# A hybrid decoder trunk: seven start offsets, 0 to 96 bytes, for the split weights in SBUF

## The chip, the cores and the metric

The kernel runs on one core of a Trainium2 chip. The metric is the device time of one execution in microseconds (us): a median of 1567.96 over 3 runs, which lie between 1567.52 and 1570.27.

## What is computed

Two layers, each: a half-step SwiGLU FFN, a token-mixing sub-layer (a Mamba-2 SSD branch and a gated DeltaNet branch on the same normalised input), and another half-step FFN. All of it is float32, for 256 tokens of width 1024:

```python
h = h + 0.5 * swiglu(rms_norm(h, ffn1_norm[l]), ffn1_w_in[l], ffn1_w_out[l])
u = rms_norm(h, mix_norm[l])
(z_s, xbc, dt_s, qkv, z_d, b_d, a_d, gate_s, gate_d) = jnp.split(u @ w_in[l], split_points, axis=-1)
y_s = mamba2_branch(z_s, xbc, dt_s, ...)
y_d = deltanet_branch(qkv, z_d, b_d, a_d, ...)
merged = (jax.nn.sigmoid(gate_s) * (y_s @ ssm_w_branch[l])
          + jax.nn.sigmoid(gate_d) * (y_d @ dn_w_branch[l]))
h = h + merged @ w_out[l]
h = h + 0.5 * swiglu(rms_norm(h, ffn2_norm[l]), ffn2_w_in[l], ffn2_w_out[l])
```

What matters here are the products with the weights: `u @ w_in`, the two FFN matrices, and the three output matrices.

## The kernel before, in words

**Split weights.** A float32 product is made from products of type fp32r. Each operand is split into a high part (the value copied into a tile of type fp32r) and a low part (the value minus its high part). A product then takes three matmuls: high by high, high by low, low by high. The weights come from HBM in half units of 128 partitions x 1024 float32 (512 KB). `load` (line 140) issues the DMA of one on the SP queue, into one of 5 `wraw` buffers, or for the first of each group of FFN output blocks into a slot (`wfirst`). `prep` (line 149) then splits a half unit: ScalarE (ACT) copies it to `hi` (line 162), VectorE (DVE) subtracts to get `lo` (line 169). `hi` and `lo` are tiles `whi` and `wlo` with NSPL = 5 buffers each. For the FFN output blocks `prep` also forms differences of half units in place (lines 163 to 171). `take` (line 181) hands out the next pair and keeps 5 pairs split ahead and the loads a few further ahead; the order is that of a plan (lines 99 to 133), and an order written out by hand (`ORDER`, line 44) for the mixer. ACT, DVE and POOL helpers are at lines 65 to 77, so most operations show lines 66 (ACT), 69 and 72 (DVE).

**The users of the split weights** are four kinds of matmul groups:

- `tok_chunk` (line 296, matmuls at lines 287 to 289 through `mm3`): the normalised input uT is stationary, the weights stream as the moving operand, 512 columns. Tiles `t` and `f`.
- `out_chunks` and `block_products` (lines 353 and 391, the same lines 287 to 289): gate products or branch outputs (`gh`/`gl`, `mh`/`ml`, `bh`/`bl`, block sums) are stationary, the weights stream, 512 columns. Tiles `o`, `b` and `p`.
- `chan_chunk` (line 313, lines 292 to 294 through `mm3w`): the weights are stationary (128x128 pieces), uT streams, 256 columns. Tiles `kk`, `qq`, `vv`, `zd`, `bc`, `xs`.
- `chan_pair` (line 332, lines 342 and 346): the FFN's input product. The high weights are stationary for 512 columns (the high and the low part of uT together), the low weights for 256.

Every matmul is preceded by a weight load (LDWEIGHTS, PEld in the profile) of its stationary operand; TensorE issues the load of the next weights while the current matmul streams.

**Placing.** Tiles are allocated pool by pool along the partition: constants, h and uT; then the pool of the weights (`wraw`, `whi`, `wlo`); then the slots (`gh`, `gl`, `mh`, ...); then small temporaries (`bh`, `bl`, ...). Each `whi` and `wlo` buffer has 4096 bytes per partition and starts on a multiple of 128 bytes. uT starts at byte 32928, which is 32 more than a multiple of 64.

Of the kernel before, what the change touches and what calls it, by code (L numbers as in the profile page):

```python
# [8 lines left out]
F32R = mybir.dt.float32r  # L9
I32 = mybir.dt.int32  # L10
AF = mybir.ActivationFunctionType
ALU = mybir.AluOpType
# [4 lines left out]
P = 128  # L17
# [13 lines left out]
NSPL = 5  # L31
# [20 lines left out]
def trunk_kernel(ctx, tc, x, wst, wsm, norms, lpar, rpar, cst, out):  # L52
# [4 lines left out]
    wpool = ctx.enter_context(tc.tile_pool(name="wpool", bufs=1))  # L57
# [7 lines left out]
    def act(o, i, func=AF.Copy, **kw):  # L65
        return A.activation(out=o, in_=i, func=func, **kw)  # L66

    def tt(o, a, b, op):
        return V.tensor_tensor(out=o, in0=a, in1=b, op=op)  # L69
# [9 lines left out]
    def f(ap):  # L79
        return ap.bitcast(F32)  # L80
# [67 lines left out]

    def prep(i):
        kind, js, _ = plan[i]  # L150
        hi = wpool.tile([P, 1024], F32R, tag="whi", name="whi", bufs=NSPL)
        lo = wpool.tile([P, 1024], F32R, tag="wlo", name="wlo", bufs=NSPL)

        def less(o, a, b):
            tt(raws[js[o]][:], raws[js[a]][:], raws[js[b]][:], ALU.subtract)


        r = raws[js[{"q2": 1, "q4": 4, "q5": 3}.get(kind, 0)]]
        with ExitStack() as behind:
            for ins in state["behind"].pop(i, ()):  # L160
                behind.enter_context(tc.issue_after(ins))
            act(hi[:], r[:])
            if kind == "q1":
                less(1, 2, 1)
            elif kind == "q2":
                less(0, 2, 0)
            elif kind == "q4":
                less(0, 3, 0)
            tt(lo[:], r[:], f(hi[:]), ALU.subtract)
            if kind == "q0":  # L170
                less(0, 1, 0)
        for o in {"d": (0,), "q2": (1,), "q3": (2,), "q4": (4,), "q5": (3,), "q6": (0,)}.get(kind, ()):
            raws.pop(js[o])
        halves[i] = (hi, lo)
# [6 lines left out]
    def take():  # L181
        j = state["taken"]
        state["taken"] = j + 1
        ahead("loaded", min(plan[min(j + NSPL, n_forms) - 1][2] + NRAW - 1, n_raw), load)
        ahead("prepped", min(j + 1 if state["hold"] else j + NSPL, n_forms), prep)
        return halves.pop(j)
# [46 lines left out]
    def rstd_of(t):  # L233

        ss = small([P, 2], "ss")
        for n in range(2):
            junk = tmp2("junk")
            state["square"] = act(junk[:], h[:, t, n * 512 : (n + 1) * 512], AF.Square, scale=1.0 / 32.0, accum_out=ss[:, n : n + 1])
        z = small([P, 2], "zz")
        ts(z[:, 0:1], ss[:, 0:1], ss[:, 1:2], ALU.add, EPS, ALU.add)  # L240
        rsqrt(z[:, 1:2], z[:, 0:1], [P, 1])
        return z[:, 1:2]
# [18 lines left out]
    def norm_in(nw, add=None):  # L261

        for t in range(2):
            with tc.high_priority(offset=PRI), ExitStack() as behind:
                if add:
                    add(t)
                    if t == 0:
                        behind.enter_context(tc.issue_after(state["sums"][5].ins))
                ins, done = rms_chain(t, nw)
            if t == 0:  # L270
                state["hold"] = False
                n = state["taken"]
                if not add:
                    ahead("prepped", n + 1, prep)
                    with tc.issue_after(done[0].ins), tc.issue_after(done[1].ins):
                        ahead("prepped", n + START, prep)
                with tc.issue_after(ins.ins):
                    ahead("prepped", n + 2, prep)
                if add:
                    state["behind"][n + 2] = [d.ins for d in done]  # L280
            elif add:

                state["behind"][n + 4] = (state["square"].ins, ins.ins)
                state["input"] = done
# [946 lines left out]
    for t in range(2):  # L1231
# [5 lines left out]
        r = rstd_of(t)  # L1237
# [137 lines left out]
```

## Time and profile before

| what | value |
|---|---|
| median of 3 runs | 1567.96 us |
| span of the profiled execution, from first to last instruction | 1565.8 us |
| PE matmul busy | 1545.0 us |
| PEld (weight loads) busy | 1342.0 us |
| DVE busy | 1302.4 us |
| ACT busy | 999.8 us |
| POOL busy | 53.2 us |
| DMA: bytes, mean rate | 292.99 MB, 187 GB/s |
| mean granted TensorE clock | 0.999 |

The profiled execution has no time of its own beside its span; the runs' median lies 2.2 us above the span. Busy times are sums over instructions. PE's instructions are pipelined, so their busy time overlaps that of the next; the distance from the start of one to the start of the next, the pitch, is what a stream of matmuls costs. A row of the timeline holds the start in us from the span's beginning, the time taken, the engine, line, operation, output and inputs, and the shape.

### The profile page before, as it was taken

The numbers are of one execution on the slowest core, as the hardware profiler recorded it, in microseconds if no ns is written. First come the engines' busy times: TensorE is split into PE (matmuls) and PEld (weight loads), VectorE is DVE, ScalarE is ACT, GpSimd is POOL, SyncE is SP. The second block draws the span as 40 slices with busy tenths as digits, with TensorE's granted clock in tenths as the row PEclk, the third lists the DMA queues.
The fourth block names the chain that finished last, engine by engine and source line by source line (L and its number), as shares of the span: only waits on it lengthen the run. The fifth ranks groups of instructions, "written<-read, shape, count | busy, mean of one in ns | idle before, by whom it ended". The sixth has DMA issues, their size and how long they took to land.

```text
span 1565.8 us, 26672 instructions
## 1 busy us (share of the span) xinstructions
PE 1545.0 (99%) x10152; PEld 1342.0 (86%) x10152; DVE 1302.4 (83%) x2048; ACT 999.8 (64%) x1694; POOL 53.2 (3%) x60
## 2 busy tenths in 40 slices
PE   8999999999999999999999999999999999999998
PEld 6888779999888888888788887899998888888886
DVE  6889969957899766899878998699579996679897
ACT  6666668766675655666566676686656666466664
POOL 0000010000000000000000001010000000000000
PEclk9999999999999999999999999999999999999999
DMA  8565565553455555465765566555336546555553
GB/s 298 197 214 188 195 212 173 178 158 118 174 207 173 177 205 196 159 210 177 262 204 187 168 198 223 189 189 189 116 123 213 177 166 212 201 175 166 198 189 134
DMA packets 94215, 292.99 MB, mean 187 GB/s; under 512 B 22325, under 2 KB 23301, under 8 KB 93062
## 3 DMA queue, kind: packets, MB, share of 16 engines
q1 hardware_dynamic: 94086, 291.29, 55.2%
q8 instruction: 79, 1.29, 0.3%
q14 instruction: 50, 0.41, 0.1%
HBM read 289.33 MB, written 1.92 MB: 186 GB/s over the span
## 4 chain that ended last, share of the span: by engine, by line
PE 76%; DVE 13%; DMA 5%; issue 3%; ACT 2%; POOL 1%; SPq 0%; POOLq 0%; DVEq 0%; ACTq 0%
PE fc L342 15%; PE fc L346 8%; DVE wlo L69 7%; PE t L287 3%; PE t L288 3%; PE t L289 3%; DMA wraw<-in_wst_dram 3%; PE b L289 3%; PE b L288 3%; PE b L287 2%; PE xs L292 2%; PE xs L293 2%; PE xs L294 2%; PE o L288 1%; PE o L289 1%
## 5 line engine op out<-in xcount | busy, mean ns | idle before, releaser
L69 DVE TENSOR_TENSOR wlo<-wraw,whi 128x1024 fp32r<-128x1024 f32 x488 | 591.0, 1221 | 139.8 <-ACT whi L66 136.1
L66 ACT ACTIVATE whi<-wraw 128x1024 fp32r<-128x1024 f32 x488 | 511.6, 1057 | 176.4 <-PE b L289 29.8
L342 PE MATMUL fc<-uT,whi 128*128 128x512 f32 x1280 | 445.5, 391 | 0.0
L346 PE MATMUL fc<-uT,wlo 128*128 128x256 f32 x1280 | 360.9, 282 | 0.0
L342 PEld LDWEIGHTS fc<-uT,whi 128*128 128x128 f32 x1280 | 240.3, 188 | 50.7
L346 PEld LDWEIGHTS fc<-uT,wlo 128*128 128x128 f32 x1280 | 241.8, 189 | 0.8
L287 PE MATMUL t<-whi,uT 128*128 128x512 f32 x256 | 102.9, 403 | 0.0
L288 PE MATMUL t<-wlo,uT 128*128 128x512 f32 x256 | 101.5, 396 | 0.2 <-DVE wlo L69 0.2
L289 PE MATMUL t<-whi,uT 128*128 128x512 f32 x256 | 101.5, 397 | 0.0
L66 ACT ACTIVATE whi<-wfirst 128x1024 fp32r<-128x1024 f32 x64 | 67.8, 1059 | 29.7 <-DVE wfirst L69 20.4
L66 ACT ACTIVATE sg<-fc 128x256 f32<-128x256 f32 x80 | 30.6, 382 | 82.3 <-PE fc L346 82.3
L69 DVE TENSOR_TENSOR wlo<-wfirst,whi 128x1024 fp32r<-128x1024 f32 x64 | 78.1, 1220 | 2.0 <-ACT whi L66 1.9
L287 PE MATMUL b<-whi,bh 128*128 128x512 f32 x192 | 76.1, 398 | 0.0
L288 PE MATMUL b<-wlo,bh 128*128 128x512 f32 x192 | 74.9, 390 | 0.0
L289 PE MATMUL b<-whi,bl 128*128 128x512 f32 x192 | 74.3, 394 | 0.3 <-DVE bl L69 0.3
L292 PE MATMUL xs<-uT,whi 128*128 128x256 f32 x256 | 73.1, 286 | 0.0
L294 PE MATMUL xs<-uT,wlo 128*128 128x256 f32 x256 | 71.6, 280 | 0.0
L293 PE MATMUL xs<-uT,whi 128*128 128x256 f32 x256 | 71.4, 279 | 0.0
L288 PE MATMUL o<-wlo,gh 128*128 128x512 f32 x160 | 64.6, 404 | 2.6 <-DVE wlo L69 2.5
L69 DVE TENSOR_TENSOR wfirst<-wraw,wfirst 128x1024 f32<-128x1024 f32 x48 | 58.6, 1220 | 8.9 <-DMA wraw<-in_wst_dram 8.9
L289 PE MATMUL o<-whi,gl 128*128 128x512 f32 x160 | 62.5, 391 | 0.0
L287 PE MATMUL o<-whi,gh 128*128 128x512 f32 x160 | 62.1, 392 | 0.0
(317 smaller groups left out, 3424.5 us busy)
## 6 DMA issues: line engine op xcount, KB each, us to landing
wraw<-in_wst_dram SPq DMA_DIRECT2D x504, 512.0 KB, 4.5
wfirst<-in_wst_dram SPq DMA_DIRECT2D x16, 512.0 KB, 5.8
dc<-rdram SPq DMA_DIRECT2D x8, 1024.0 KB, 8.4
nw<-in_norms_dram SPq DMA_DIRECT2D x6, 512.0 KB, 6.2
gb<-rdram SPq DMA_DIRECT2D x8, 256.0 KB, 5.3
h<-in_x_dram SPq DMA_DIRECT2D x4, 256.0 KB, 5.7
out_dram<-fo SPq DMA_DIRECT2D x4, 256.0 KB, 2.1
dq<-X SPq DMA_DIRECT2D x2, 256.0 KB, 5.0
```

Source lines behind the costliest of these rows:

```text
L66: return A.activation(out=o, in_=i, func=func, **kw)
L69: return V.tensor_tensor(out=o, in0=a, in1=b, op=op)
L287: PE.matmul(ps, lh, rh, start=start, stop=False)
L288: PE.matmul(ps, lh, rl, start=False, stop=False)
L289: return PE.matmul(ps, ll, rh, start=False, stop=stop)
L292: PE.matmul(ps, wh, mh, start=start, stop=False)
L293: PE.matmul(ps, wh, ml, start=False, stop=False)
L294: PE.matmul(ps, wl, mh, start=False, stop=stop)
L342: PE.matmul(ps[a][:], wh[:, c0 : c0 + P], uT[:, kt].rearrange("p o t -> p (o t)"), start=kt == 0, stop=False,)
L346: PE.matmul(ps[a][:, 0:S], wl[:, c0 : c0 + P], uTh[:, kt, :], start=False, stop=kt == KT - 1)
```

## The change

The `whi` and `wlo` buffers get 24 elements (96 bytes) more per partition, and the 1024 elements in use start at an offset into the buffer: 16 bytes times (i mod 7) for the high part and 16 bytes times ((i div 7) mod 7) for the low part, where i counts the half units split so far. So the high part goes through 0, 16, ..., 96 bytes with each half unit, and the low part changes every seventh. The buffers are 4192 bytes apart instead of 4096, so they no longer all start on a multiple of 128; the slots and temporaries behind them move by 960 bytes. `hi` and `lo` are now views of the tiles, so the later uses lose their `[:]`.

```diff
     def prep(i):
         kind, js, _ = plan[i]
-        hi = wpool.tile([P, 1024], F32R, tag="whi", name="whi", bufs=NSPL)
-        lo = wpool.tile([P, 1024], F32R, tag="wlo", name="wlo", bufs=NSPL)
+        o1, o2 = 4 * (i % 7), 4 * (i // 7 % 7)
+        hi = wpool.tile([P, 1024 + 24], F32R, tag="whi", name="whi", bufs=NSPL)[:, o1 : o1 + 1024]
+        lo = wpool.tile([P, 1024 + 24], F32R, tag="wlo", name="wlo", bufs=NSPL)[:, o2 : o2 + 1024]
...
-            act(hi[:], r[:])
+            act(hi, r[:])
...
-            tt(lo[:], r[:], f(hi[:]), ALU.subtract)
+            tt(lo, r[:], f(hi), ALU.subtract)
```

## The prediction

> **What bounds the kernel now.** The page's busy table and clock row come first, then the chain that ended last, then the costliest groups.
>
> ```profile
> span 1565.8 us, 26672 instructions
> PE 1545.0 (99%) x10152; PEld 1342.0 (86%) x10152; DVE 1302.4 (83%) x2048; ACT 999.8 (64%) x1694; POOL 53.2 (3%) x60
> PEclk9999999999999999999999999999999999999999
> ...
> PE 76%; DVE 13%; DMA 5%; issue 3%; ACT 2%; POOL 1%; SPq 0%; POOLq 0%; DVEq 0%; ACTq 0%
> ...
> L69 DVE TENSOR_TENSOR wlo<-wraw,whi 128x1024 fp32r<-128x1024 f32 x488 | 591.0, 1221 | 139.8 <-ACT whi L66 136.1
> L66 ACT ACTIVATE whi<-wraw 128x1024 fp32r<-128x1024 f32 x488 | 511.6, 1057 | 176.4 <-PE b L289 29.8
> L342 PE MATMUL fc<-uT,whi 128*128 128x512 f32 x1280 | 445.5, 391 | 0.0
> L346 PE MATMUL fc<-uT,wlo 128*128 128x256 f32 x1280 | 360.9, 282 | 0.0
> ```
>
> PE is busy 99% of the span at full granted clock, and PE work is 76% of the chain. DVE and ACT, which make the split weights, stand on 15% of it. So TensorE sets the time, and what counts is how far apart its matmuls start. The "mean ns" of a matmul (391) is no help: it holds a pipelined tail. The pitch is read from the timeline of PE, from the first and the last row of runs without a break (only matmuls of the run stand between): `o` over 39 steps, `t` over 70, `zd` and `bc` over 93, `fc` over 112.
>
> ```profile
> 591.11 0.39 PE L289 MATMUL o<-whi,ml 128*128 128x512 f32 x1
> ...
> 599.95 0.39 PE L289 MATMUL o<-whi,ml 128*128 128x512 f32 x1
> ```
> ```profile
> 505.55 0.40 PE L288 MATMUL t<-wlo,uT 128*128 128x512 f32 x1
> ...
> 521.88 0.40 PE L289 MATMUL t<-whi,uT 128*128 128x512 f32 x1
> ```
> ```profile
> 319.76 0.28 PE L292 MATMUL zd<-uT,whi 128*128 128x256 f32 x1
> ...
> 330.61 0.28 PE L292 MATMUL bc<-uT,whi 128*128 128x256 f32 x1
> ```
> ```profile
> 633.94 0.39 PE L342 MATMUL fc<-uT,whi 128*128 128x512 f32 x1
> ...
> 653.35 0.39 PE L342 MATMUL fc<-uT,whi 128*128 128x512 f32 x1
> ```
>
> The pitches: `o` 8.84/39 = 226.7 ns; `t` 16.33/70 = 233.3 ns for the same 512 columns; `zd`/`bc` 10.85/93 = 116.7 ns for 256 columns; `fc` 19.41/56 = 346.6 ns for a pair of one 512 and one 256. From `o` and `zd`: 110.0 ns for 256 more columns, 0.43 ns a column, and 6.7 ns left over in each matmul.
>
> The change moves addresses only, so I ask what an address does here. By the program's own allocation every whi and wlo buffer starts on a multiple of 128 bytes, so do gh, gl, mh, ml, bh and bl, but uT starts 32 bytes past a multiple of 64. In `o`, moving operand (whi, wlo) and stationary operand (gh or the like) both start on a multiple of 64. In `t` the moving one does and the stationary one (uT) is 32 off: 6.7 ns dearer. In `zd` and `fc` the stationary one (whi, wlo) is on 64 and the moving one (uT) is 32 off. That is all the evidence: no fp32r operand now starts 16 or 48 past a multiple of 64.
>
> After the change the buffers are 4192 bytes apart and the offsets 0 to 96 are added. Counted over the 7936 fp32r matmuls, 28% of the starts of whi and wlo lie on a multiple of 64, 28% 32 off, and 44% (3468) 16 or 48 off. The slots and temporaries behind them move by 960 bytes, to 64 past a multiple of 128. Order and waits of the instructions stay the same on every engine.
>
> **The change part by part.** Nothing is removed or added. The terms are counts times a change of pitch:
>
> ```profile
> 0.00:1566.00 1566.00, 254.06 (x896) 168.45 (x896) 1.00 0.56 187
> ```
> ```profile
> L288 PEld LDWEIGHTS t<-wlo,uT 128*128 128x128 f32 x256 | 48.1, 188 | 11.8 <-DVE wlo L69 0.7 <-DVE ca L72 0.5
> L289 PEld LDWEIGHTS o<-whi,gl 128*128 128x128 f32 x160 | 30.1, 188 | 5.5
> L287 PE MATMUL f<-whi,uT 128*128 128x512 f32 x64 | 26.4, 415 | 0.5 <-ACT uT L66 0.5
> ```
>
> The first row is line 292 alone over the span; lines 293, 294 and 287 to 289 have 896 each too. So there are 3 x 896 = 2688 matmuls of 256 columns with split weights as stationary (the channel units), 2688 of 512 with them as moving operand, of which 3 x (256 + 64) = 960 take uT (`t`, `f`) and 1728 gh, bh, mh and the like (`o`, `b`, `p`), and 2 x 1280 in the FFN.
>
> A. *Weight loads under a 512-column matmul.* The load of the next weights runs while the current matmul streams. In the FFN the load of wlo (line 346) runs under the 512 columns of line 342; 75% of these loads leave the multiple of 64. Price: what uT's 32 bytes seem to cost in `t`, 233.3 - 226.7 = 6.7 ns. 0.75 x 1280 x 6.7 = +6.4 us. Ends: 0 (the two LDWEIGHTS rows take 188 ns each, on 64 or not) and 6.7 ns.
>
> B. *Weight loads under 256 columns* (2688 and the FFN's 1280, 70% of them off: 2776). No row shows a misaligned load there. From below -3.3 ns (half of the 6.7 ns left over), from above +6.7 (the price in `t`): -9.2 to +18.6 us. I take 0: these matmuls already stream a misaligned uT, and their 6.7 ns left over is no more than that of `o`.
>
> C. *Moving operand off 64 in `o`, `b`, `p`.* 73% of 1728 = 1256. uT is a misaligned moving operand in `fc`, whose pair takes 346.6 ns against 226.7 + 116.7 = 343.4: 3.3 ns. 1256 x 3.3 = +4.1 us. Ends: 0, and 5.8 ns, for after a wait the same matmuls run at 0.93/4 = 232.5 ns for a while (five of them here, the first two in one row), so the 226.7 looks like a lock that can be lost: +7.3 us.
>
> ```profile
> 181.11 0.62 PE L287 MATMUL o<-whi,gh 128*128 128x512 f32 x2
> ...
> 182.04 0.39 PE L287 MATMUL o<-whi,gh 128*128 128x512 f32 x1
> ```
>
> D. *Moving operand off 64 in `t`, `f`* (960, 72%: 692). They pay for uT already: 0 taken; ends -6.7 and +3.3 ns, -4.6 to +2.3 us.
>
> E. *ACT and DVE writing and reading at the offsets, DMA into moved slots.* DVE already works at 4, 8 and 12 bytes past a line in the convolution (`ca[:, j:]`, j = 1 to 3), each for its 255, 254 or 253 elements:
>
> ```profile
> L72 DVE SCALAR_TENSOR_TENSOR ca<-xs,lp,ca 128x255 f32<-128x255 f32 x32 | 15.2, 478 | 1.9 <-ACT ca L66 1.9
> L72 DVE SCALAR_TENSOR_TENSOR ca<-xs,lp,ca 128x254 f32<-128x254 f32 x32 | 15.1, 476 | 0.1
> L72 DVE SCALAR_TENSOR_TENSOR ca<-xs,lp,ca 128x253 f32<-128x253 f32 x32 | 15.0, 475 | 0.1
> L69 DVE TENSOR_TENSOR tg<-tg,mt 128x512 f32<-128x512 f32 x8 | 5.3, 683 | 0.0
> L69 DVE TENSOR_TENSOR fo<-h,nw 128x512 f32<-128x512 f32 x4 | 2.8, 692 | 0.1
> ...
> wfirst<-in_wst_dram SPq DMA_DIRECT2D x16, 512.0 KB, 5.8
> ```
>
> 478, 476 and 475 ns: no price. The widest gap is `fo`, one input 32 off: 692 against 683, 9 ns. On 552 subtractions that is 5.0 us of DVE, hidden beneath PE except for DVE's 13% of the chain: 0.6 us at most, 0 taken. Of the loads only the 16 into slots get another start; their 5.8 us lies beneath the matmuls; if it were late by a tenth each, 16 x 0.6 = 9 us would still be covered by the loads issued ahead. 0 taken.
>
> *Sum.* A + C = +10.5 us of PE work. Where weights come late, a slower PE only waits less, so I count the chain's PE share, 76%: +8.0 us. The span is 1565.8 and the median of the runs, 1567.96, lies 2.2 above it, which I leave as it is: 1568 + 8 = **1576 us**. Upper ends: 6.4 + 18.6 + 7.3 + 2.3 = 34.6 us, 26.3 with the 76%: 1594.
>
> **A rule that speaks against any effect.** The pitches above are the row: 226.7, 233.3 and 116.7 ns. The Trainium skill, page "TensorE: Matmul & The Clock Gate", section "Step-by-step: what each phase is for", says that TensorE reads SBUF through two independent ports, one for the streamed operand and one for the weight load; its section "Wait — 56ns, not 53.3ns?" gives a matmul N/2.4 + about 2.5 ns, so by that page an estimate of 215.8 ns for 512 columns. And the page "SBUF — State Buffer", section "Specifications (TRN2)", has lines of 16 bytes, of which every offset here is a multiple. By both the change costs nothing. The trace agrees only in part: `t` and `o`, alike but for the stationary start, are 6.7 ns apart, and both are above that estimate.
>
> **The rivals.**
>
> 1. *No effect.* The 6.7 ns of `t` come from something else than uT's 32 bytes, and contiguous 16-byte steps are all alike. For: the loads take 188 ns in both; `fc` and `zd` run well with a misaligned uT. Then 1568.
>
> 2. *Every misaligned load pays*, under 256 columns too. For: the one clean difference in the trace. Against: `zd` shows no room, its left-over is 6.7 ns already. A + C + B's upper end = 29.1 us, 22.1 with the 76% or 29.1 without: 1590 to 1597.
>
> 3. *Faster: the even starts are the bad case.* The 6.7 ns left over per matmul are collisions between the load's reads and the stream's reads, which march over the same lines because all starts agree modulo 32; a start 16 or 48 off lets them pass each other. For: the pitches are strictly periodic, and the 232.5 after a wait shows that phase matters. Against: `t`, whose two starts differ by 32, is dearer and not cheaper. 3468 x 6.7 ns = 23.2 us, 17.7 with the 76%: 1550 at its best, 1559 with half of it. It decides once a freed load gives more than A + C spread over the 3468 freed ones, 10.5/3468 = 3.0 ns each.
>
> That the offsets don't reach the hardware is excluded: the starts differ in the program as counted.
>
> **How the numbers follow.** Forecast (1571 to 1588) 0.37; every load pays 0.17; no effect 0.18; faster 0.28. A measurement of this kernel tells about 0.2% (3.1 us) from no change, which is the bound of the chances: faster 0.28, same 0.18, slower 0.37 + 0.17 = 0.54. The range goes from 1552, nearly all of rival 3, to 1598, the end of rival 2.
>
> **What would show it.** In the trace after: `fc` pairs at 346.6 ns (no effect), about 350 (A: 0.75 x 6.7 = 5.0 on the pair), 356 (rival 2) or below 343 (rival 3); `zd` at 116.7 for A and C, about 121.5 for rival 2; `o` runs at 228 to 231 instead of a steady 226.7; `t` unchanged at 233.3. The pitch should change between runs with the offset of the weights in use; if it doesn't, no address matters and A and C both fall. The wlo subtraction should stay at 1221 ns and whi's copy at 1057; a rise there by over 50 ns would put DVE's 552 subtractions on the path in the stages that wait for wlo, and would make the prediction wrong by a mechanism that I gave nothing.

## The result, and the profile after

The changed kernel takes **1577.61 us** (median of 3 runs, 1577.54 to 1579.46) against 1567.96 before: a ratio of 1.0057, with a 95% interval of 1.0039 to 1.0075. It is slower by 9.65 us.

The page of the changed kernel, the lines that answer to those of before (the diff adds a line, so 342 is now 343):

```profile
span 1577.7 us, 26672 instructions
PE 1555.8 (99%) x10152; PEld 1344.4 (85%) x10152; DVE 1303.1 (83%) x2048; ACT 1001.6 (63%) x1694; POOL 52.1 (3%) x60
PEclk9999999999999999999999999999999999999999
...
PE 82%; DVE 8%; DMA 5%; ACT 2%; issue 2%; POOL 0%; SPq 0%; POOLq 0%; ACTq 0%; DVEq 0%
...
L69 DVE TENSOR_TENSOR wlo<-wraw,whi 128x1024 fp32r<-128x1024 f32 x488 | 591.0, 1221 | 145.4 <-ACT whi L66 143.4
L66 ACT ACTIVATE whi<-wraw 128x1024 fp32r<-128x1024 f32 x488 | 513.0, 1058 | 184.0 <-PE b L290 31.8
L343 PE MATMUL fc<-uT,whi 128*128 128x512 f32 x1280 | 448.9, 394 | 0.0
L347 PE MATMUL fc<-uT,wlo 128*128 128x256 f32 x1280 | 358.2, 280 | 0.0
...
wfirst<-in_wst_dram SPq DMA_DIRECT2D x16, 512.0 KB, 5.8
```

DVE and ACT do the same work in the same time: 1221 ns for a low part as before, 1058 against 1057 ns for a high part. The clock is the same. PE is busy 10.8 us longer, its part of the chain goes from 76 to 82%, and DVE's falls from 13 to 8%: the matmuls are slower, and the weights come late for less of the time. So the time went where the prediction looked, into the pitch. Runs from the timeline of PE in the changed kernel: `o` over 96 steps, `t` over 70, `zd` over 47, `fc` over 96 (48 pairs):

```profile
940.15 0.39 PE L288 MATMUL o<-whi,bsc 128*128 128x512 f32 x1
...
962.35 0.62 PE L288 MATMUL o<-whi,gh 128*128 128x512 f32 x2
```
```profile
509.13 0.39 PE L289 MATMUL t<-wlo,uT 128*128 128x512 f32 x1
...
525.29 0.39 PE L290 MATMUL t<-whi,uT 128*128 128x512 f32 x1
```
```profile
322.19 0.28 PE L293 MATMUL zd<-uT,whi 128*128 128x256 f32 x1
...
327.76 0.28 PE L295 MATMUL zd<-uT,wlo 128*128 128x256 f32 x1
```
```profile
30.98 0.28 PE L347 MATMUL fc<-uT,wlo 128*128 128x256 f32 x1
...
47.74 0.28 PE L347 MATMUL fc<-uT,wlo 128*128 128x256 f32 x1
```

`o` 22.20/96 = 231.3 ns (226.7 before), `t` 16.16/70 = 230.9 (233.3), `zd` 5.57/47 = 118.5 (116.7), an `fc` pair 16.76/48 = 349.2 (346.6). Single runs differ by a nanosecond or so. From here on I use means over a whole group: from start to start, over all matmuls that are followed by another matmul with split weights, whose stationary operand is already being loaded (so without the waits). Before and after, in ns, and what the difference makes over all the matmuls of the group:

| group | before | changed | matmuls | us |
|---|---|---|---|---|
| `o`, `b`, `p` (512 columns) | 227.7 | 231.9 | 1728 | +7.3 |
| `t`, `f` (512) | 233.1 | 231.9 | 960 | -1.2 |
| channel units (256) | 116.8 | 118.3 | 2688 | +4.0 |
| `fc`, high weights (512) | 228.6 | 232.1 | 1280 | +4.4 |
| `fc`, low weights (256) | 118.3 | 117.5 | 1280 | -1.0 |

The sum is +13.5 us. The span grew by 11.9 and the median by 9.65; the profiled execution of the changed kernel was the slowest of its three, 1579.46 us. Of the 1.6 us between pitch and span, 1.3 show as waits: the weight loads waited for a low part for 11.7 us before and for 10.4 after.

### The profile page after: what moved, and what is told of

It is laid out like the page before. It is cut to its first block, busy times and chain, and to the rows that moved or that the text cites. A ratio compares the mean times of both kernels' runs of the same rounds, so it can differ in the third digit from the quotient of the medians.

```text
span 1577.7 us, 26672 instructions
## 1 busy us (share of the span) xinstructions
PE 1555.8 (99%) x10152; PEld 1344.4 (85%) x10152; DVE 1303.1 (83%) x2048; ACT 1001.6 (63%) x1694; POOL 52.1 (3%) x60
## 4 chain that ended last, share of the span: by engine, by line
PE 82%; DVE 8%; DMA 5%; ACT 2%; issue 2%; POOL 0%; SPq 0%; POOLq 0%; ACTq 0%; DVEq 0%
PE fc L343 17%; PE fc L347 9%; DVE wlo L69 4%; PE t L289 3%; PE t L288 3%; PE t L290 3%; DMA wraw<-in_wst_dram 3%; PE b L290 3%; PE b L289 3%; PE b L288 3%; PE o L290 2%; PE o L289 2%; PE xs L293 2%; PE xs L294 2%; PE xs L295 2%
## 5 line engine op out<-in xcount | busy, mean ns | idle before, releaser
L69 DVE TENSOR_TENSOR wlo<-wraw,whi 128x1024 fp32r<-128x1024 f32 x488 | 591.0, 1221 | 145.4 <-ACT whi L66 143.4
L66 ACT ACTIVATE whi<-wraw 128x1024 fp32r<-128x1024 f32 x488 | 513.0, 1058 | 184.0 <-PE b L290 31.8
L66 ACT ACTIVATE whi<-wfirst 128x1024 fp32r<-128x1024 f32 x64 | 67.7, 1058 | 31.3 <-DVE wfirst L69 19.6
```

## The experiments

Two theories stood at the start. *Price per start*, the prediction's own: a matmul pays for an operand that starts off a multiple of 64 bytes. *Lost rhythm*: a steady run of equal starts falls into a good cycle, and a mixture spoils it. The first fell. The second fell as the whole account, though part of it holds for the mixtures, as the traces show further below. A third was added, the *price of the distance*: the pitch hangs on the distance between the start of the operand that streams and the start of the one that is loaded beside it. A distance is given here as the start of uT, or of the slot, less that of the weights.

### The padding alone

```diff
-        o1, o2 = 4 * (i % 7), 4 * (i // 7 % 7)
+        o1 = o2 = 0
```

> The buffers are 96 bytes longer, as in the changed kernel, but every offset is 0: the starts still lie on 0, 32, 64 or 96 past a multiple of 128 by the buffer in use, none at 16 or 48 past a multiple of 64. Theory 'lost rhythm' (a steady run of equal starts lets load and stream fall into a short repeating cycle; any mixture of starts spoils it, and the pitch goes to about 232 ns for 512 columns and 118 ns for 256, whatever the single start is): nearly the time of the changed kernel, 1574 to 1578 us, out pitch 231 to 232 ns. Theory 'price per start' (a start off a multiple of 64 costs something in each matmul, as in A and C of the prediction): 40% of the starts are off instead of 72%, so about 0.55 of the loss, 1571 to 1574 us, and the 60% that lie on 64 keep 226.7 ns. Theory 'the odd sixteens': no loss, 1568 us.

1582.78 us, ratio 1.0075 (1.0058 to 1.0092). That is no smaller a loss than the whole change, with no start at 16 or 48. `o` takes 231.8 ns, a pair of `fc` 349.0, the channel units 119.1. So the offsets are not needed for the loss: that the buffers are 4192 bytes apart and the slots 960 bytes further is enough. The price per start had asked for half the loss, so it looked doubtful here. (By the program's own allocation 48% of the matmuls have a weight start off a multiple of 64, not the 40% of the expectation; that is still short of the whole loss.)

### The weights' starts back on a multiple of 128

```diff
-        o1, o2 = 4 * (i % 7), 4 * (i // 7 % 7)
+        o1, o2 = 8 * (0, 0, 3, 2, 1)[i % NSPL], 8 * (1, 1, 0, 3, 2)[i % NSPL]
```

> The buffers are 96 bytes longer, and each gets one fixed offset that puts its start back on a multiple of 128; the starts of the five buffers still differ modulo 512, and the slots lie 64 bytes further, as in the changed kernel. Price per start: all starts on a multiple of 64, so 1568 us and 226.7 / 346.6 / 116.7 ns as before. Lost rhythm: if the rhythm depends on starts modulo 128 or less, 1568 us too; if it depends on more address bits, it stays lost, 1574 to 1578 us and 232 / 118 ns. A result of 1568 lets both stand, a result near 1577 rules out the price per start.

1575.73 us, ratio 1.0034 (1.0021 to 1.0047). The weights and the slots start on multiples of 64 again (uT stays 32 off), and `o` still takes 231.4 ns, `t` 233.4, a pair 348.5, the channel units 117.7. The price per start is ruled out for `o`. Lost rhythm could still stand, but so could the 64 bytes by which the slots lie further.

### The input on a multiple of 128

```diff
+    uT = cpool.tile([P, KT, 2, S], F32R, name="uT")
     mhalf = cpool.tile([P, 1], F32, name="mhalf")
...
-    uT = cpool.tile([P, KT, 2, S], F32R, name="uT")
```

> The kernel before, but the normalised input uT is allocated first, on a multiple of 128, so that every fp32r operand starts on a multiple of 128 (and equal modulo 512 to the weights' buffers). Price per start: t falls from 233.3 to 226.7 ns (960 x 6.7 = 6.4 us), the fc pair from 346.6 to 343.4 (1280 x 3.2 = 4.1 us): 1557 to 1562 us. Lost rhythm: t now has the relation of starts that o has and takes 226.7 ns; fc and the channel units settle in another cycle whose length nothing here shows, 340 to 352 ns a pair and 113 to 120 ns: 1550 to 1575 us. If uT's 32 bytes have nothing to do with t's 233.3 ns, 1568 us.

1580.73 us, ratio 1.0067 (1.0052 to 1.0082). Every operand starts on a multiple of 128 now, and the kernel is slower, where the price per start had asked for 6 to 11 us less. Timeline of this kernel, `t` over 49 steps, `zd` over 47, `fc` over 96:

```profile
508.38 0.40 PE L288 MATMUL t<-wlo,uT 128*128 128x512 f32 x1
...
519.51 0.39 PE L289 MATMUL t<-whi,uT 128*128 128x512 f32 x1
```
```profile
322.44 0.28 PE L292 MATMUL zd<-uT,whi 128*128 128x256 f32 x1
...
328.07 0.28 PE L294 MATMUL zd<-uT,wlo 128*128 128x256 f32 x1
```
```profile
30.93 0.28 PE L346 MATMUL fc<-uT,wlo 128*128 128x256 f32 x1
...
47.90 0.28 PE L346 MATMUL fc<-uT,wlo 128*128 128x256 f32 x1
```

`t` falls to 11.13/49 = 227.1 ns, as forecast: its 233.3 ns were indeed uT's 32 bytes. But `zd` rises to 5.63/47 = 119.8 and a pair of `fc` to 16.97/48 = 353.5. No starts are mixed, so lost rhythm has no reason for it either, beyond "another cycle". What changed for all three is the distance between weights and input, from 32 to 0: cheaper when the input is loaded, dearer when it streams.

### A scan of the input's start

```diff
+    room = cpool.tile([P, KT * 2 * S + 64], F32R, name="uT")
+    shifts = iter(SHIFTS)
...
     def norm_in(nw, add=None):
+        k = next(shifts) // 4
+        uT = room[:, k : k + KT * 2 * S].rearrange("p (k o t) -> p k o t", k=KT, o=2)
```

> The kernel before with uT starting 0 bytes (first FFN), 0 (first mixer), 16 (second FFN), 64 (third FFN), 16 (second mixer) and 48 bytes (fourth FFN) past a multiple of 128, one fixed start in each stage: a look at the pitches of a steady run at each start, no timing. Price per start: 0 and 64 alike and best, 16 and 48 alike, fc pairs between 343 and 347 ns. Lost rhythm: each stage has a steady pitch of its own with little scatter, in either direction from 346.6 and 116.7 ns, 16 and 48 need not be worse than 0, and none has the scatter of the changed kernel.

One execution: 1577.13 us. The first FFN and the first mixer (0) repeat the kernel above: a pair 353.1, channel units 119.9, `t` 227.7. At 16 bytes the pair is 346.9 and the channel units 118.1, at 48 the pair 346.9, at 64 350.6. So 16 and 48 are no worse than 32 (346.9 before), and 64 differs from 0: the modulus is more than 64. The whole scan, with two later ones, is in a table below.

### The slots 64 bytes further

```diff
     wpool = ctx.enter_context(tc.tile_pool(name="wpool", bufs=1))
+    gpool = ctx.enter_context(tc.tile_pool(name="gpool", bufs=1))
+    gpool.tile([P, 16], F32, name="gap")
     slots = ctx.enter_context(tc.tile_pool(name="slots", bufs=1))
```

> The kernel before with one empty 64-byte tile between the weights' buffers and the slots: gh, mh and the like (stationary in o, b, p) start 64 past a multiple of 128, all else has the starts of before. Theory 'price of the distance' (the pitch is set by the distance, modulo 128 or more, between the start of the operand that is loaded and that of the operand that streams; a mixture costs the mean over its distances): out goes from 227.7 to about 231 to 233 ns, as t at distance 64 in the scan (233.3) and out in the kernel realigned (231.4): 1727 x 4 to 5.6 ns = +7 to +10 us over the kernel before; t, fc and the channel units unchanged. Theory 'mixing costs' (what hurts is that starts differ from one matmul to the next): nothing is mixed here, no more than +2 us.

1576.66 us, ratio 1.005 (1.0035 to 1.0065). `o` over 87 steps of its timeline, 20.29/87 = 233.2 ns:

```profile
158.84 0.39 PE L289 MATMUL o<-whi,bsc 128*128 128x512 f32 x1
...
179.13 0.39 PE L289 MATMUL o<-whi,gh 128*128 128x512 f32 x1
```

The mean of `o`, `b` and `p` goes from 227.7 to 233.2 ns; `t` (233.2), the pairs (346.7) and the channel units (116.8) stay as they were. An empty tile of 64 bytes costs nearly as much as the whole change, with all the weights where they were and nothing mixed. Lost rhythm falls here as the whole account: a steady run can be dear too.

### Realigned, with the slots put back

```diff
     wpool = ctx.enter_context(tc.tile_pool(name="wpool", bufs=1))
+    gpool = ctx.enter_context(tc.tile_pool(name="gpool", bufs=1))
+    gpool.tile([P, 16], F32, name="gap")
...
+        o1, o2 = 8 * (0, 0, 3, 2, 1)[i % NSPL], 8 * (1, 1, 0, 3, 2)[i % NSPL]
```

> The kernel realigned with the slots put back on a multiple of 128 by the same 64-byte tile: padding of 96 bytes stays, all starts are those of before modulo 128, but the five buffers still differ modulo 512. Price of the distance modulo 128: out back to about 227.5 ns, within 0 to +3 us of the kernel before. Price of the distance modulo 512, or mixing: out stays at 231 ns, +5 to +7 us as in realigned.

1577.45 us, ratio 1.0056 (1.0041 to 1.0071); `o` 230.9 ns in the group's mean, and 20.75/90 = 230.6 in a run of its timeline:

```profile
160.19 0.40 PE L290 MATMUL o<-whi,bsc 128*128 128x512 f32 x1
...
180.94 0.39 PE L290 MATMUL o<-whi,gh 128*128 128x512 f32 x1
```

The forecast by a modulus of 128 missed. Either distances of 0 and 128 differ, or the turns between the buffers cost (a turn is a change of distance from one matmul to the next).

### The slots 128 bytes further

```diff
+    gpool.tile([P, 32], F32, name="gap")
```

> As slots_64, but the empty tile has 128 bytes: the stationary operands of o, b and p lie 128 further from the weights, modulo 512, and no start is mixed. Price of the distance modulo 128, plus a price of mixing (the theory now, since realigned_slots kept 231 ns with every distance a multiple of 128 but changing from buffer to buffer): out 227.7 ns and the time of the kernel before, within 2 us. Price of the distance modulo 512: out 230 to 232 ns, as in realigned_slots, and +5 to +7 us.

1575.83 us, ratio 1.0036 (1.0021 to 1.0052). `o` over 90 steps, 20.91/90 = 232.3 ns; the group's mean is 232.5:

```profile
159.56 0.39 PE L289 MATMUL o<-whi,bsc 128*128 128x512 f32 x1
...
180.47 0.39 PE L289 MATMUL o<-whi,gh 128*128 128x512 f32 x1
```

The theory as I had it by then, modulus 128 plus a price of mixing, missed again: nothing is mixed, and a distance of 128 is nearly as dear as one of 64. The modulus is 256 or more. That it is not 512 is suggested by kernels that were there already: uT at a distance of 256 from the weights (the scan's first stages) and at 0 (the kernel with the input on 128) have the same pitches, pairs of 353.1 and 353.1, channel units 119.9 and 119.9, `t` 227.8 and 227.6. In `realigned_slots` 47% of the `o` matmuls lie at 0 and 53% at 128 modulo 256, and 0.47 x 227.7 + 0.53 x 232.5 = 230.2 against the measured 230.9. The means come close, but the turns are not free. With the start addresses of the program's allocation set beside the records of the trace, the matmuls at 0 take 230.5 ns there, not 227.7, and those at 128 take 231.3, not 232.5. A run at one distance is only some six matmuls long, and it settles slowly:

| `o` matmuls at distance 0 | before, ns | `realigned_slots`, ns |
|---|---|---|
| first three after a break or a turn | 232.1 | 231.1 |
| next three | 228.5 | 229.3 |
| from the seventh on | 226.9 | 226.7 (18 records) |

At distance 0 a turn costs as a wait does: the pitch begins at 231 to 232 ns and needs about six matmuls to come down to 227.

### The offsets alone, by turns and held

```diff
-        hi = wpool.tile([P, 1024 + 24], F32R, tag="whi", name="whi", bufs=NSPL)[:, o1 : o1 + 1024]
-        lo = wpool.tile([P, 1024 + 24], F32R, tag="wlo", name="wlo", bufs=NSPL)[:, o2 : o2 + 1024]
+        hi = wpool.tile([P, 1024 + 32], F32R, tag="whi", name="whi", bufs=NSPL)[:, o1 : o1 + 1024]
+        lo = wpool.tile([P, 1024 + 32], F32R, tag="wlo", name="wlo", bufs=NSPL)[:, o2 : o2 + 1024]
...
-    one = cpool.tile([1, P], F32, name="one")
+    one = s2.tile([1, P], F32, tag="s2", name="one")
```

> The offsets of the change exactly (0 to 96 bytes, the high part's with each half unit, the low part's with each seventh), but in buffers 4224 bytes apart, so that every buffer's base and every slot stays on a multiple of 128. (The 512 bytes of a small constant tile are taken from a temporary to make room.) Price of the distance: out 231 to 232, t 231 to 232, fc pairs 349, channel units 118.3: +8 to +12 us, the loss of the changed kernel without its moved bases and slots. If the bases and slots were the whole loss: 0 to +3 us.

1580.40 us, ratio 1.0074 (1.0059 to 1.0089): the offsets lose as much as the padding alone, and neither adds to the other (`o` 231.9, `t` 231.8, a pair 349.4, channel units 118.2, all as in the changed kernel). The second kernel has, besides,

```diff
-        o1, o2 = 4 * (i % 7), 4 * (i // 7 % 7)
+        o1 = o2 = 4 * (i // 20 % 7)
```

> As offsets_alone, but both parts have the same offset, and each of the seven is held for 20 half units (some 160 matmuls) before the next. Price of the distance: each held stretch has a steady pitch of its own, t 227.6 at the offset of 32 (distance 0) and 231 to 233 elsewhere, fc pairs 353 at 32, 347 at 0 and 16; the time is the mean over them, within 3 us of offsets_alone. Mixing costs: the held stretches run at the best pitch of each group, 226.7 / 347 / 117, and the time is 5 us or more below offsets_alone.

1579.52 us, ratio 1.0061 (1.0041 to 1.0082), 0.9 us from the one by turns. Holding an offset does not help. This says nothing for or against a price of mixing: the stretches weren't steady as I had expected, because buffers 4224 bytes apart alternate by 128 modulo 256, which I did not yet count as different. For the same reason `offsets_alone` is not the offsets strictly alone.

### The rest of the scan, and a version from it

Both kernels have the scan's code with other starts.

```diff
-SHIFTS = (0, 0, 16, 64, 16, 48)
+SHIFTS = (80, 64, 96, 112, 96, 128)
```

> The scan with uT starting 80 bytes (first FFN), 64 (first mixer), 96 (second FFN), 112 (third FFN), 96 (second mixer) and 128 (fourth FFN) past a multiple of 128, steady in each stage: a look at pitches. Price of the distance modulo 128: the fourth FFN's pairs 353 ns as at 0 in the first scan; the channel units at 64 near 114 ns, as the stretches of offsets_held at that distance (714 matmuls at 114.1), at 96 near 118; fc pairs at 80, 96, 112 between 345 and 351. If only mixing counted: all alike.

One execution: 1581.00 us. The last FFN, at 128, has pairs of 350.9 ns and `t` at 233.1, not the 353.1 and 227.7 of 0: 128 and 0 differ for the input too. The channel units at 64 took 117.1, not 114.

```diff
-SHIFTS = (0, 0, 16, 64, 16, 48)
+SHIFTS = (32, 64, 32, 32, 64, 32)
```

> The kernel before with uT starting 32 bytes past a multiple of 128 in the FFNs, as before, and 64 bytes past one in the two mixers. Price of the distance: the channel units go from 116.8 to about 114 ns, 2688 x 2.7 = 7 us less; t stays at 233.3, fc and out as before: 1560 to 1564 us, faster than both kernels. If the 114 ns of offsets_held came from its mixture: 116 to 119 ns, within 3 us of the kernel before.

1571.15 us, ratio 1.0012 (1.0003 to 1.0021): not faster. The channel units take 117.3 ns. The 114.1 ns that had pointed here belonged to stretches in which high and low weights lay 64 bytes on opposite sides.

```diff
-SHIFTS = (0, 0, 16, 64, 16, 48)
+SHIFTS = (144, 192, 176, 208, 224, 240)
```

> The other half of the distances: uT starts 144 bytes (first FFN), 192 (first mixer), 176, 208 (second and third FFN), 224 (second mixer) and 240 (fourth FFN) past a multiple of 128, counted on to 256. Price of the distance modulo 256 with a mixture paying the mean: the changed kernel's means (t 231.9, fc pairs 349.6, channel units 118.3) must come out as means over all sixteen distances; with the nine seen so far (t 232.3, fc pairs 350.2, channel units 118.4 over five) the new ones must lie around t 231.4, fc pairs 349 (single values from 344 to 354), channel units 116 to 120. If the channel units at 192 show about 111 ns, the 114 ns of offsets_held (buffers that lie 64 on either side by turns) is the mean of 117 and 111. If mixing has a price of its own of over 3 ns, the new means lie that far below the changed kernel's.

One execution: 1571.27 us, beside 1570.95 for the kernel before. At 192 the channel units run at 115.0 ns in the mean, below the 116.8 of before, though unevenly: `kk` over 95 steps of this timeline takes 10.85/95 = 114.2, `zd` over 47 steps 5.54/47 = 117.9.

```profile
233.27 0.36 PE L298 MATMUL kk<-uT,whi 128*128 128x256 f32 x1
...
244.12 0.28 PE L300 MATMUL kk<-uT,wlo 128*128 128x256 f32 x1
...
318.56 0.28 PE L298 MATMUL zd<-uT,whi 128*128 128x256 f32 x1
...
324.10 0.28 PE L300 MATMUL zd<-uT,wlo 128*128 128x256 f32 x1
```

The mean of 117.2 (at 64) and 115.0 (at 192) is 116.1, so the 114.1 of the alternating stretches is not their mean. The unevenness at 192 has a pattern: each unbroken run of the first mixer settles to one of two paces, near 113.3 ns or near 117.8, with the same starts modulo 256. So the distance alone does not fix the pitch of the channel units. Most of the alternating stretches of `offsets_held` also stand near 113.3. What puts a run on one pace or the other, no run shows.

All starts of uT, in bytes past the weights' own start modulo 256, with mean pitches in ns (32 is the kernel before; the `t`, `f` values at 80 and 144 rest on some 30 matmuls each):

| start | `t`, `f` | `fc` pair | channel units |
|---|---|---|---|
| 0 | 227.7 | 353.1 | 119.9 |
| 16 | 231.3 | 346.9 | 118.1 |
| 32 | 233.1 | 346.9 | 116.8 |
| 48 | 233.2 | 346.9 | |
| 64 | 233.3 | 350.6 | 117.2 |
| 80 | 232.2 | 353.1 | |
| 96 | 234.1 | 350.1 | 119.9 |
| 112 | 233.1 | 353.2 | |
| 128 | 233.1 | 350.9 | |
| 144 | 233.1 | 346.7 | |
| 176 | 230.0 | 350.0 | |
| 192 | 229.3 | | 115.0 |
| 208 | 231.8 | 352.1 | |
| 224 | 233.2 | | 118.3 |
| 240 | 227.9 | 353.0 | |
| mean | 231.8 | 350.3 | 117.9 |
| changed kernel | 231.9 | 349.6 | 118.3 |

The last two rows: the changed kernel, whose starts go through all the distances, runs at the mean over them, to within 0.7 ns. This agreement is one of means and does not hold matmul by matmul. In the changed kernel the `o`, `b`, `p` matmuls at distance 0 take 231.2 ns, those at 64 take 231.8 and those at 128 take 231.6, where the steady kernels show 227.7, 233.2 and 232.5. The distance turns there every few matmuls, and the pitch stays near 232 whatever it is. That is what lost rhythm had said of a mixture; what it lacked is that a steady run at another distance is as dear.

One limit remains. In every steady kernel the weights start at 128 modulo 256, so a distance and a start of the other operand go together. The start of the weights counts as well: in `offsets_alone` the slots and uT keep their starts modulo 256, and `o` rises to 231.9 ns. That only the difference of the two counts, no run shows.

And the sums of the pitches, worked out for each kernel as for the changed one above, follow the measured times to within 2.2 us, but for the changed kernel (3.9) and `realigned` (5.3), whose rest is only partly explained:

| kernel | sum of pitches, us | median less that of before, us |
|---|---|---|
| changed | +13.5 | +9.65 |
| pad_only | +14.7 | +12.8 |
| realigned | +11.0 | +5.7 |
| input_on_128 | +11.4 | +10.7 |
| slots_64 | +9.2 | +7.9 |
| realigned_slots | +10.0 | +8.7 |
| offsets_alone | +12.7 | +11.7 |
| offsets_held | +10.8 | +10.8 |
| slots_128 | +7.9 | +6.4 |
| input_64_in_mixers | +1.6 | +1.7 |
| input_scan (one execution) | +6.1 | +7.1 |
| input_scan_2 (one execution) | +11.8 | +11.5 |
| input_scan_3 (one execution) | +2.5 | +0.3 |

The scan points to uT at 192 in the mixers and 32 in the FFNs: (116.8 - 115.0) x 2688 + (233.1 - 229.3) x 768 `t` matmuls = 7.7 us less, an estimate from its rows. That kernel was not run, so whether it beats both is open; the like estimate for `input_64_in_mixers` did not come true.

## Why the prediction was right, and where its reasons were wrong

The time came out at 1577.6 against 1576, with the sign and the place right: the pitch of the split matmuls, nothing on ACT or DVE. The reason given, a price for a start off a multiple of 64, was wrong.

- **The bound.** Right. PE is the limit, and its pitch, not its busy time, is what to read. I had let 76% through, the PE share of the chain. Of +13.5 us of pitch, 88% reached the span of the profiled execution and 71% the median, so the share was about right. DVE's part of the chain fell from 13 to 8%.
- **A, loads under the 512 columns of `fc`: +6.4 us.** The high-weight matmuls, under which these loads run, did rise, by 3.4 ns: +4.4 us. The price I had carried over from `t`, 6.7 ns for uT's 32 bytes, is that of a distance of 32 against one of 0, for an input that is loaded. With the weights loaded and the input streaming, the same 32 is among the best distances found for the pair (346.9 ns) and 0 among the worst (353.1).
- **B, loads under 256 columns: 0, ends -9.2 and +18.6.** The channel units rose by 1.5 ns, +4.0 us, and the low-weight matmuls of `fc`, which the term counts too, fell by 0.8, -1.0 us: +3.0, inside the ends. I took 0 because "these matmuls already stream a misaligned uT"; in truth the channel units stood at a good distance (116.8 of a range from 115.0 to 119.9), and the mixture cost them.
- **C, `o`, `b`, `p`: +4.1 us.** Mis-sized: 4.2 ns on all 1728 is +7.3 us, at the upper end that I had from the disturbed stretch (232.5 ns, +7.3). That end had the better reason, "a lock that can be lost": `o` stood at distance 0, the cheapest for a loaded activation, and the runs no longer settle there. 92% of the group left distance 0, not the 73% that left a multiple of 64, and the 8% that kept it rose as well, to 231.2 ns.
- **D, `t` and `f`: 0.** -1.2 us: `t` stood at a dear distance and gained by the mixture.
- **E, ACT, DVE, DMA: 0.** Right: 1221 and 1058 ns, wfirst 5.8 us.
- **Rival 1, no effect**, was excluded by the measurement; **rival 2, every misaligned load pays**, by `input_on_128`, where nothing is misaligned and the time is 10.7 us longer, and by `pad_only`. **Rival 3** had one true point, that the starts of the two operands matter together, and the wrong sign: the starts of before were on the whole a good case. Its reason, collisions of reads, no run tests.

That the sum came within 2 us is partly luck: A was too high by 2.0, B, C and D together were too low by 5.0, and the prices came from a wrong reason.

What showed it wrong was named in the prediction ("t unchanged at 233.3", "zd at 116.7"): both moved. It named another sign, that the pitch should change with the offset of the weights in use, or else "A and C both fall". In the changed kernel the `o`, `b`, `p` matmuls whose weights start on a multiple of 64 take 231.7 ns, those 16 off 231.4, 32 off 232.6 and 48 off 231.9. None keeps 227.7, and being off costs 0.9 ns at most, where C had asked for 3.3. So by its own sign the price per start falls.

The prediction weighed two statements of the Trainium skill. Its page "TensorE: Matmul & The Clock Gate", section "Step-by-step: what each phase is for", gives TensorE one read port for the streamed operand and another, independent, for the weight load. By that, where the loaded operand lies could not matter to the stream; but `slots_64` moved only the loaded operand, by 64 bytes, and the pitch went from 227.7 to 233.2 ns. And the lines of 16 bytes on the page "SBUF — State Buffer", section "Specifications (TRN2)", would make all these starts alike; the kernels, which differ in multiples of 16 alone, lie between 1568 and 1583 us. The measurements decide against both as a bound on this cost.

## What to carry to other kernels

Where a kernel is bound by a dense stream of fp32r matmuls, the placing of tiles in SBUF is worth some 0.7% here, without a single instruction changed: a new small tile or a longer buffer can cost more than an edit gains, so compare the pitch of steady runs before blaming the edit. Keep the distance between the two operands of a matmul group the same for all buffers, and choose it by measuring: a steady run takes some six matmuls to settle here, and a mixture that turns sooner does not. Spreading the starts over many offsets ran at about the mean over the distances (231.9 against 231.8 ns for `t`).

## What the runs showed of the hardware

- The steady pitch of fp32r matmuls with alternating weight loads hangs on the distance of the two operands' starts: 64 and 128 differ from 0 by 4.8 to 5.6 ns at 512 columns. A period of 256 bytes fits: 0 and 256 agree to 0.2 ns. The best distance is not the same for all orders of matmuls: 0 for activations loaded and weights streaming (227.7 ns against up to 234.1), 16 to 48 (and 144) for the FFN's pairs (346.7 to 346.9 against up to 353.2).
- A run takes time to settle: at distance 0 `o` begins at 231 to 232 ns after a wait or a turn and reaches 227 from the seventh matmul on. Under a mixture that turns sooner it stays near 232.
- At one distance two paces can occur: 113.3 and 117.8 ns for the channel units at 192.
- Why it is so, which reads meet where, no run shows.
- ACT and DVE are indifferent to starts in steps of 16 bytes: 1057 to 1058 ns and 1221 ns for 1024 columns.
